# One visit per batch instead of four: grouping the value matmuls of a paged-attention loop

## The chip, the cores and the metric

The kernel runs on one core of one Trainium2 chip. Its time is the device time of one execution in microseconds (us). TensorE does the matmuls (PE in the profile, with PEld for the loads of its stationary operand), VectorE is DVE, ScalarE is ACT, GpSimd is POOL, and the queue that issues nearly all transfers is SP.

## The reference, cut to what matters

One step of a decoder layer is computed for 1024 prompt tokens and for eight samples of four new tokens each. The stage changed here is the attention of the samples over their cached past: 4096 positions in 32 pages of 128, for each of eight samples, with eight heads.

```python
def one(args):
    pages, q1, c1, pe1 = args
    c_all = jnp.concatenate([pool_ckv[pages].reshape(PAST_LEN, KV_LORA), c1.astype(pool_ckv.dtype)], axis=0)
    pe_all = jnp.concatenate([pool_kpe[pages].reshape(PAST_LEN, QK_ROPE), pe1.astype(pool_kpe.dtype)], axis=0)
    k, v = mla_keys_values(c_all, pe_all, k_pos, w_uk, w_uv, g_qk_k)
    return masked_attend(q1, k, v, q_pos, k_pos)
```

Keys are RMS-normalised per head after the projection, so each key needs the sum of squares of its 96 values. The kernel does not form the values v: it sums the cached latents with the softmax weights first and multiplies by `w_uv` once at the end.

## The kernel before

The score loop has 128 steps, 16 for each of the eight samples ("batches" 0 to 7 in the code). Four pages make a quad, so a batch has eight quads and a step handles half a quad. Everything in the loop is written out by hand in the function `steps`: for PE, ACT, DVE and POOL the order of the instructions is the order of the code, and work that belongs to a step is put there with `at(n, pos, f)`; only the order on SP is chosen by the scheduler. After step 127 a tail follows (steps 128 to 147 together with `mem_kv`, the keys and values of the prompt's memory) in which the scheduler orders every engine but SP.

In step n, `pair_score` issues 24 score matmuls into the tiles `s` and `s2` (two buffers each; both are called `s` in the profile). ACT squares both (`sq`, two buffers, lines 1452 and 1455), DVE adds the scores to `S` (line 1454) and in the next step reduces the squares to `ss` (line 1458). Every two steps ACT rounds the next quad's transposed latents to `ch` and POOL and DVE form the remainder `cl`, half each (line 1407).

The softmax of batch b runs in steps 16b+12 to 16b+21, in pieces of `batch_softmax`: sums of squares plus the rope part (line 1469) and a reciprocal root in a dozen DVE instructions on 192 columns (lines 247 to 261), the scaling of 24 pages on POOL and the peak over them on DVE, the same for the last 8 pages, then the peak over partitions: TensorE transposes `mx` (line 1508, step 16b+19), DVE reduces it and makes the diagonal `dg` (lines 1511, 1513), TensorE spreads it with `ones` (line 1516, step 16b+20), POOL subtracts, and ACT takes the exponential in step 16b+21. Batch 0 does the same while `mix_steps`, a leftover of the prompt, runs beside it.

The value matmuls come `LAG` = 4 steps after that. `quad_pv` multiplies one quad's latents `ck` by the weights in `S`. The output has 32 rows, so four pages are put into the four 32-column groups of the array; I call a run of such matmuls, between score matmuls that use the full array, a visit. An f32 matmul leaves two records in the trace, so a quad has eight records. Line 1535 adds the new tokens (`cn`) at a batch's first quad.

Before, batch b is visited in steps 16b+23, 16b+27, 16b+31 and 16b+35, with two quads each. The last of these visits stands right behind the transpose of `mx` of batch b+1. Then `batch_out` copies the sums (line 1545), divides (lines 1549 to 1555) and `batch_close` adds up the four groups (line 1561, the fold) in steps 16b+35 to 16b+39.

The latents `ck` come into a ring of 15 buffers. The same ring lends buffers to four loads of the prompt's mixer output (`mixed_load`), which ACT and DVE later scale and split into `mx0h` and `mx0l` (lines 205 and 208), one of each in two steps. POOL writes a one into each quad's column 256 (line 1284), which makes the matmul sum up the weights too.

Of the kernel before, what the change touches and what calls it, by code (L numbers as in the profile page):

```python
# [15 lines left out]
NB, ND = 8, 4  # L16
# [138 lines left out]
class Net:  # L155
# [1024 lines left out]
    def phase2b(self):  # L1180
        nc, tc, I = self.nc, self.tc, self.I
# [4 lines left out]
        ppt, pp = self.open("ps3t", space=PSUM), self.open("ps3", space=PSUM)  # L1186
# [10 lines left out]
        cosT, sinT, quads = self.cosT, self.sinT, self.quads  # L1197

        LAG, AHEAD = 4, 3
        last = NB * 16  # L1200
        st, ev, late = {}, {}, []

        def at(n, pos, f, *a):
            ev.setdefault((n, pos), []).append(lambda: f(*a))

        def run(n, pos):
            for f in ev.pop((n, pos), []):
                f()
# [13 lines left out]
        def mixed_load(k):  # L1222

            raw = place()[:, :768].rearrange("p (k n) -> p k n", k=2)
            nc.sync.dma_start(raw, self.mix_dram[:, k : k + 2, :384])
            for e in range(2):
                at(8 * k + 24 + 2 * e, 3, lambda e: self.split(*(x[:, k + e] for x in self.mx0), raw[:, e], self.col("g_ab", k + e)), e)

        for k in range(0, 8, 2):
            at(8 * k + 20, 0, mixed_load, k)  # L1230
        at(last - 4, 3, lambda: self.split(*wk0, raws[0].rearrange("p (k n) -> p k n", k=8)))
        for b in range(NB):
            n = b * 16
            at(n - 10, 0, lambda b: st.__setitem__(b, self.batch_open(p, b)), b)
            at(n - 8, 2, lambda b: self.batch_enter(st[b], b), b)
            for r, (k, pos) in enumerate(((12, 0), (13, 0), (14, 0), (14, 3) if b == NB - 1 else (15, 0), (15, 0) if b == NB - 1 else (15, 3), (16, 0), (17, 0), (17, 3), (18, 2), (19, 2), (20, 0), (20, 2), (21, 3))):
                f = lambda b=b, r=r: self.batch_softmax(p, ppt, st[b], r, b == NB - 1)
                if n + k <= last:
                    at(n + k, pos, f)
                else:  # L1240
                    late.append(f)
            if b < NB - 1:
                at(n + 21, 0, lambda b=b: self.batch_softmax(p, ppt, st[b], 13, False))
            n += 16 + LAG + 15
            tail = (
                lambda b=b: self.batch_out(pt, st[b], 0),
                lambda b=b: self.batch_out(pt, st[b], 1, ppt, b == NB - 1),
                lambda b=b: self.batch_close(pt, ppt, b, st.pop(b)),
            )
            for k, pos, f in ((0, 3, tail[0]), (2, 2, tail[1]), (3 if b == NB - 2 else 4, 3, tail[2])):  # L1250
                if b < NB - 1:
                    at(n + k, pos, f)
# [4 lines left out]
        def steps(n0, n1):  # L1257
            for n in range(n0, n1):
                Q, v = n // 2, n - 16 - LAG
                if n >= 16 and n % 2 == 0 and Q + AHEAD < NB * 8:  # L1260
                    quads[Q + AHEAD] = self.quad_load(p, Q + AHEAD)
                for k, dst, src in ((2, b4, self.b_dram), (16, self.fold4, I["c_fold4"]), (64, wuv, I["w_uv"])):
                    if n == k:
                        self.behind(nc.sync.dma_start(dst, src), self.page_dma[-1])
                if n > last - 8 and n % 2 == 0 and len(raws) < 4:
                    raw = place()[:, : 8 * P]
                    src = (I["w_mk"][0], I["memT"][:, :4], I["memT"][:, 4:], I["w_mk"][1])[len(raws)]
                    nc.sync.dma_start(raw.rearrange("p (k n) -> p k n", n=src.shape[2]), src)
                    raws.append(raw)
                for pos in (-2, -1, 0):  # L1270
                    run(n, pos)
                if n % 2 == 0 and 0 <= Q + 1 < NB * 8:
                    at(n + 1, -2, self.quad_prep(quads[Q + 1]))
                    at((6, 8, 10, 10, 11)[Q + 1] if Q < 4 else n + 3, 0, self.quad_sums, Q + 1, quads[Q + 1], st[(Q + 1) // 8])
                if n % 2 and 0 <= Q + 2 < NB * 8:
                    self.quad_rot(Q + 2, quads[Q + 2], cosT, sinT)
                if n in (-1, 1, 3, 5, 7, 9, 11, 13):
                    k = Q + 4
                    rvs[k] = rvs.get(k) or self.quad_pages(k)
                    quads[k] = self.quad_load(None, k, None, rvs[k])  # L1280
                for k in {1: (0,), 3: (1,), 4: (2,), 5: (3,), 6: (4,), 7: (5,), 9: (6,), 11: (7,), 12: (8,), 13: (9,), 14: (10,)}.get(n, ()):
                    self.quad_load(p, k, quads[k], rvs.get(k))
                if n % 2 and 0 <= v + 1 < last:
                    nc.gpsimd.memset(quads[(v + 1) // 2]["ck"][:, :, 256:257], 1.0)
                run(n, 1)
                if 0 <= n < last:
                    rope = (Q + 1, quads[Q + 1], st[(Q + 1) // 8]) if n % 2 and Q + 1 < NB * 8 else None
                    for f in self.pair_score(p, pp, n, quads[n // 2], st[n // 16], rope):
                        at(n + 1, -1, f)
                elif n == -1:  # L1290
                    self.quad_rope(self.t(pp, [P, 2, 512], F32, "s", 2)[:, 0, 320:448], 0, quads[0], st[0])()
                run(n, 2)
                if 0 <= v < last and v % 4 == 3:
                    for z in (v // 2 - 1, v // 2):
                        self.quad_pv(ppt, z, quads.pop(z), st[v // 16])
                run(n, 3)

        with tc.manual_schedule(engines={E.PE, E.Activation, E.DVE, E.Pool}):
            steps(-10, last + 1)

        with tc.manual_schedule(engines={E.SP}):
            self.close("ps3")
            for x in ("p3a", "p3c", "sq", "sm"):
                self.close(x)
            self.wr = self.open("wr", bufs=3, side="right")
            self.wp = self.open("w", bufs=3, side="right")
            mem = self.mem_kv(raws, wk0)
            for f in late[:3]:
                f()
            next(mem)  # L1310
            steps(last + 1, last + 4)
            for _ in range(5):
                next(mem)
            steps(last + 4, last + 7)
            for f in late[3:]:
                f()
            for _ in range(6):
                next(mem)
            steps(last + 7, last + 16 + LAG)
            for _ in mem:  # L1320
                pass
# [1191 lines left out]
```

## Time and profile before

| what | value |
|---|---|
| time, median of 3 runs | 1827.49 us (1826.86 to 1828.1) |
| profiled execution, from its first to its last instruction | 1823.1 us |
| TensorE busy | 1800.6 us (99%) |
| VectorE busy | 1349.6 us (74%) |
| ScalarE, GpSimd busy | 921.5 us (51%), 703.0 us (39%) |
| score loop, first score matmul to last | 400.88 to 847.28 us |

For the profiled execution the page gives the span alone; the runs' times also hold what lies around it, 4.4 us between the span and the median. Times inside the text are counted from the start of the span. A row of the timeline reads: start, duration, engine, line, operation, output<-inputs, shape, count, and in brackets the idle time of the engine before it with what ended that. A row of a table by windows reads: stretch, its length, and each engine's busy time with the number of instructions in parentheses.

### The profile page before, as it was taken

Reading aid. Unit: us, or ns where it says so; the run is one execution under the profiler, and the core shown is the slowest. Engines: PE = TensorE matmul, PEld = TensorE weight load, DVE = VectorE, ACT = ScalarE, POOL = GpSimd, SP = SyncE. Lnnn points to the kernel's source line nnn. Section 1 sums busy time; section 2 is a strip of 40 time slices with the busy share of each in tenths; the row PEclk is TensorE's granted clock in tenths of the full one; section 3 lists DMA queues with packets and bytes.
Section 4 is the critical chain, followed back from the end, with each engine's and each line's share of the span. In section 5 each row is a group of like instructions: output and inputs, shape, how many; then the busy total and the mean of one; then the engine's idle time right before and its main releaser. Section 6 shows DMA issues by size and latency. Waiting matters only on the chain.

```text
span 1823.1 us, 39307 instructions
## 1 busy us (share of the span) xinstructions
PE 1800.6 (99%) x14226; PEld 1700.3 (93%) x14226; DVE 1349.6 (74%) x2796; ACT 921.5 (51%) x1910; POOL 703.0 (39%) x861
## 2 busy tenths in 40 slices
PE   9999999999999999999999999999999999999999
PEld 8999777779999999998899979999999999999999
DVE  7864767657778776777645767998888888888664
ACT  7435676766655555556433556533333333344442
POOL 1021655534545444544023010377667776400000
PEclk9999999999999999999999999999999999999999
DMA  8102354558866766664645156222222222595242
GB/s 323 47 18 70 117 176 127 165 181 227 220 201 189 202 189 181 178 180 127 194 152 188 36 197 196 71 71 94 83 71 71 83 71 85 152 325 162 85 149 78
DMA packets 153187, 261.18 MB, mean 143 GB/s; under 512 B 20897, under 2 KB 97538, under 8 KB 152994
## 3 DMA queue, kind: packets, MB, share of 16 engines
q1 hardware_dynamic: 152130, 257.63, 45.4%
q8 instruction: 112, 1.84, 0.4%
q10 hardware_dynamic: 864, 1.05, 0.2%
q14 instruction: 81, 0.66, 0.1%
HBM read 212.79 MB, written 45.82 MB: 142 GB/s over the span
## 4 chain that ended last, share of the span: by engine, by line
PE 81%; DVE 3%; ACT 1%; issue 1%; SPq 1%; POOL 1%; DMA 0%; DVEq 0%; ACTq 0%; POOLq 0%
PE s L186 22%; PE d L186 12%; PE b L186 8%; PE F L186 7%; PE X L186 7%; PE E L186 7%; PE A L186 3%; PE y L186 3%; PE o L1047 2%; PE o L1537 2%; PE tp L1032 1%; PE tp L186 1%; PE s L1422 1%; PE tp L985 1%; PE t L186 1%
## 5 line engine op out<-in xcount | busy, mean ns | idle before, releaser
L186 PE MATMUL s<-w2h,ch 128*128 128x256 f32 x1018 | 301.9, 297 | 0.5 <-ACT S L1425 0.5
L186 PE MATMUL s<-w2h,cl 128*128 128x256 f32 x1018 | 293.2, 288 | 0.0
L186 PE MATMUL s<-w2l,ch 128*128 128x256 f32 x1018 | 292.9, 288 | 0.0
L186 PEld LDWEIGHTS s<-w2h,ch 128*128 128x128 f32 x1018 | 191.5, 188 | 8.9 <-issue 3.7
L186 PEld LDWEIGHTS s<-w2l,ch 128*128 128x128 f32 x1018 | 191.7, 188 | 0.0
L186 PEld LDWEIGHTS s<-w2h,cl 128*128 128x128 f32 x1018 | 191.3, 188 | 0.0
L1458 DVE TENSOR_REDUCE ss<-sq 128x16 f32<-128x1024 f32 x128 | 155.3, 1213 | 29.8 <-ACT sq L1455 29.4
L1407 POOL TENSOR_TENSOR cl<-cT,ch 128x512 fp32r<-128x512 f32 x64 | 83.5, 1304 | 185.6 <-ACT ch L1403 185.4
L1455 ACT ACTIVATE sq<-s 128x512 f32<-128x512 f32 x128 | 76.6, 598 | 82.7 <-PE s L186 82.7
L1452 ACT ACTIVATE sq<-s 128x512 f32<-128x512 f32 x128 | 76.9, 601 | 75.9 <-PE s L186 70.9
L201 ACT CAST a<-brb 128x528 fp32r<-128x528 f32 x77 | 48.8, 634 | 110.5 <-PE d L186 104.6
L186 PE MATMUL d<-a,w 128*128 128x264 f32 x768 | 95.2, 284 | 0.0
L202 DVE TENSOR_TENSOR a<-brb,a 128x528 fp32r<-128x528 f32 x77 | 54.1, 704 | 55.2 <-ACT a L201 55.1
L186 PEld LDWEIGHTS d<-a,w 128*128 128x128 f32 x768 | 94.3, 188 | 0.0
L2149 POOL TENSOR_TENSOR lo<-s,hi 128x1024 fp32r<-128x1024 f32 x20 | 64.0, 3200 | 45.7 <-ACT hi L2148 45.7
L186 PE MATMUL mm<-whi,xh 128*128 128x256 f32 (+3 forms) x272 | 77.1, 285 | 0.0
L2204 ACT COPY a<-A 128x264 f32<-128x264 f32 x43 | 16.1, 375 | 120.6 <-PE A L186 114.2
L186 PE MATMUL mm<-wlo,xh 128*128 128x256 f32 (+3 forms) x272 | 76.8, 285 | 0.1
L186 PE MATMUL mm<-whi,xl 128*128 128x256 f32 (+3 forms) x272 | 76.8, 286 | 0.0
L1403 ACT CAST ch<-cT 128x512 fp32r<-128x512 f32 x128 | 73.5, 629 | 0.0
L2270 POOL TENSOR_TENSOR cv<-cv,row 128x1056 f32<-128x1056 f32 x22 | 65.1, 2960 | 21.0 <-ACT cv L2269 21.0
L186 PE MATMUL d<-a,hi 128*128 128x264 f32 x552 | 72.0, 284 | 0.0
(755 smaller groups left out, 6348.1 us busy)
## 6 DMA issues: line engine op xcount, KB each, us to landing
cT<-cT SPq DMA_DIRECT2D x256, 160.0 KB, 2.8
ck<-ck SPq DMA_DIRECT2D x256, 144.0 KB, 3.4
raw<-w_up SPq DMA_DIRECT2D x44, 512.0 KB, 3.5
wsumd<-wsum SPq DMA_DIRECT2D x26, 512.0 KB, 3.9
actd<-cv SPq DMA_DIRECT2D x44, 264.0 KB, 2.4
brb<-actd SPq DMA_DIRECT2D x44, 264.0 KB, 5.7
wsum<-w_down SPq DMA_DIRECT2D x22, 512.0 KB, 3.8
raw<-wsumd SPq DMA_DIRECT2D x20, 512.0 KB, 3.7
```

The costliest lines, as they stand in the source:

```text
L186: x = self.nc.tensor.matmul(out, l, r, start=first and i == 0, stop=last and i == len(seq) - 1)
L201: first = {"act": nc.scalar.copy, "pool": nc.gpsimd.tensor_copy, "dve": nc.vector.tensor_copy}[eng](hi, src)
L202: low = lambda: nc.vector.tensor_tensor(lo, src, hi, ALU.subtract)
L1047: nc.tensor.matmul(u["o"][g : g + 64, o : o + m * P], s["v"][:, j, h % 4], th[:, z * P : (z + m) * P], start=j == 0, stop=b == len(banks) - 1,
L1403: nc.scalar.copy(d["h"][:, k], src[k])
L1407: (nc.vector if k else nc.gpsimd).tensor_tensor(d["l"][:, k], src[k], d["h"][:, k], ALU.subtract)
L1452: nc.scalar.activation(sq[:, 0], ps[:, :, n0 : n0 + 256], AF.Square)
L1455: nc.scalar.activation(sq[:, 1], pt.rearrange("p (e d) -> p e d", e=2), AF.Square)
L1458: yield lambda: nc.vector.tensor_reduce(s["ss"][:, g0 : g0 + 2].rearrange("p e (z h) -> p z e h", z=2), sq.rearrange("p z e (h d) -> p z e ...
L1537: nc.tensor.matmul(s["o"][j * 32 : j * 32 + 32], S[:, q * 4 + j], d["ck"][:, j, :257], start=q == 0 and j > 0, stop=q == 7)
L2149: eng.tensor_tensor(lo, src, hi, ALU.subtract)
L2270: nc.gpsimd.tensor_tensor(cv, cv, row, ALU.mult)
```

## The change

All eight quads of a batch are now multiplied in one visit, in step 16b+23. Batch 6 keeps two quads back: six in step 119, and two that the code places in step 131, in the tail. With the last quads done, `batch_out` and the fold follow in steps 16b+23 to 16b+27 instead of 16b+35 to 16b+39 (batch 6 keeps its place). The memset of column 256 is moved 12 steps earlier. The four mixed loads and their splits are moved four steps later: loads from steps 20, 36, 52, 68 to 24, 40, 56, 72, and splits from steps 24 and 26 (40 and 42, and so on) to 28 and 30 (44 and 46, and so on).

```diff
             for e in range(2):
-                at(8 * k + 24 + 2 * e, 3, lambda e: self.split(*(x[:, k + e] for x in self.mx0), raw[:, e], self.col("g_ab", k + e)), e)
+                at(8 * k + 28 + 2 * e, 3, lambda e: self.split(*(x[:, k + e] for x in self.mx0), raw[:, e], self.col("g_ab", k + e)), e)
 
         for k in range(0, 8, 2):
-            at(8 * k + 20, 0, mixed_load, k)
+            at(8 * k + 24, 0, mixed_load, k)
...
-            n += 16 + LAG + 15
+            n += 16 + LAG + (15 if b == NB - 2 else 3)
...
-                if n % 2 and 0 <= v + 1 < last:
-                    nc.gpsimd.memset(quads[(v + 1) // 2]["ck"][:, :, 256:257], 1.0)
+                if n % 2 and 0 <= n - 7 < last:
+                    nc.gpsimd.memset(quads[(n - 7) // 2]["ck"][:, :, 256:257], 1.0)
...
-                if 0 <= v < last and v % 4 == 3:
-                    for z in (v // 2 - 1, v // 2):
-                        self.quad_pv(ppt, z, quads.pop(z), st[v // 16])
+                if 0 <= v < last and v % 16 in (3, 15):
+                    b, held = v // 16, 2 if v // 16 == NB - 2 else 0
+                    for z in range(b * 8, b * 8 + 8 - held) if v % 16 == 3 else range(b * 8 + 8 - held, b * 8 + 8):
+                        self.quad_pv(ppt, z, quads.pop(z), st[b])
```

Here v is n - 16 - LAG. Lines behind the loop have a number one higher afterwards.

TensorE around the transpose of batch 3's peaks (step 67), before:

```order
L186 MATMUL s_1635_10295<-w2l_1706,ch_10111 128x256
L186 MATMUL s_1635_10295<-w2h_1705,cl_10112 128x256
L1508 MATMUL m_10325<-ident_60,mx_10051 32x128
L1537 MATMUL o_9494<-ck_8291,S_7186 32x257 x4
L1537 MATMUL o_9494<-ck_8434,S_7186 32x257 x4
L186 MATMUL s_10396<-w2h_1705,ch_10245 128x288
L186 MATMUL s_10396<-w2l_1706,ch_10245 128x288
```

The same place in TensorE's order afterwards:

```order
L186 MATMUL s_1638_10319<-w2l_1706,ch_10135 128x256
L186 MATMUL s_1638_10319<-w2h_1705,cl_10136 128x256
L1509 MATMUL m_10349<-ident_60,mx_10075 32x128
L186 MATMUL s_10408<-w2h_1705,ch_10269 128x288
L186 MATMUL s_10408<-w2l_1706,ch_10269 128x288
```

The eight value matmuls that stood between the transpose and the scores of step 68 are gone from there, and the transpose stands alone.

VectorE at the beginning of batch 3's softmax (steps 60 and 61), before:

```order
L1469 TENSOR_TENSOR ss_8299<-ss_8299,kss_8300 128x192
L247 TENSOR_SCALAR rqx_1578_9824<-ss_8299 128x192
L248 TENSOR_SCALAR rqy_1580_9826<-rqx_1578_9824 128x192
L249 TENSOR_SCALAR rqy_1580_9826<-rqy_1580_9826 128x192
L1454 TENSOR_TENSOR S_8298<-s_9835,S_8298 128x64
L1407 TENSOR_TENSOR cl_9832<-cT_9544,ch_9831 128x512
L1458 TENSOR_REDUCE ss_8299<-sq_9861 128x2x2x4
```

The same place in VectorE's order afterwards:

```order
L1470 TENSOR_TENSOR ss_8306<-ss_8306,kss_8307 128x192
L247 TENSOR_SCALAR rqx_1581_9852<-ss_8306 128x192
L248 TENSOR_SCALAR rqy_1583_9854<-rqx_1581_9852 128x192
L249 TENSOR_SCALAR rqy_1583_9854<-rqy_1583_9854 128x192
L1455 TENSOR_TENSOR S_8305<-s_9863,S_8305 128x64
L208 SCALAR_TENSOR_TENSOR mx0l_5691<-ck_9586,cols_58,mx0h_5690 128x384
L1408 TENSOR_TENSOR cl_9860<-cT_9574,ch_9859 128x512
L1459 TENSOR_REDUCE ss_8306<-sq_9889 128x2x2x4
```

A mixed split (line 208) now stands ahead of the remainder `cl`, and a second one does so two steps later; before, both came in the steps ahead of this stretch.

VectorE in the second half of the reciprocal root of the last batch (around step 126), before:

```order
L256 SCALAR_TENSOR_TENSOR rqa_2077_14173<-rqy_2076_14172 128x192
L259 TENSOR_TENSOR rqa_2077_14173<-rqa_2077_14173,rqx_2074_14170 128x192
L260 SCALAR_TENSOR_TENSOR rqh_2075_14171<-rqa_2077_14173 128x192
L261 SCALAR_TENSOR_TENSOR ss_12752<-rqh_2075_14171,rqy_2076_14172 128x192
L1454 TENSOR_TENSOR S_12751<-s_14263,S_12751 128x64
```

The same place in VectorE's order afterwards:

```order
L256 SCALAR_TENSOR_TENSOR rqa_2077_14187<-rqy_2076_14186 128x192
L1552 RECIPROCAL rd_14458<-m_14456 128x1
L259 TENSOR_TENSOR rqa_2077_14187<-rqa_2077_14187,rqx_2074_14184 128x192
L1556 TENSOR_SCALAR oo_14408<-oo_14408,rd_14458 128x256
L260 SCALAR_TENSOR_TENSOR rqh_2075_14185<-rqa_2077_14187 128x192
L261 SCALAR_TENSOR_TENSOR ss_12761<-rqh_2075_14185,rqy_2076_14186 128x192
L1455 TENSOR_TENSOR S_12760<-s_14277,S_12760 128x64
```

The division of batch 6's sums now stands inside the root, ahead of the last additions to `S`; before, it came after them. On TensorE the scheduler puts batch 6's two held quads not into the tail but between score matmuls of steps 122 to 126, in three pieces of 2, 2 and 4 matmuls.

## The prediction

> **What bounds the kernel now.** I read the page first, then TensorE's timeline at the visits, then VectorE's rows in the softmax steps.
>
> ```profile
> span 1823.1 us, 39307 instructions
> PE 1800.6 (99%) x14226; PEld 1700.3 (93%) x14226; DVE 1349.6 (74%) x2796; ACT 921.5 (51%) x1910; POOL 703.0 (39%) x861
> PE 81%; DVE 3%; ACT 1%; issue 1%; SPq 1%; POOL 1%; DMA 0%; DVEq 0%; ACTq 0%; POOLq 0%
> ```
>
> TensorE is busy 99% of the span and makes 81% of the chain that ended last, so an interval taken from it counts unless another engine then makes it wait. The mean hides that the engines take turns in being nearly full. A table by windows, for steps 12 to 19 of batches 0, 3 and 5, shows it:
>
> ```profile
> 439.23:466.13 26.90, 26.68 (x217) 26.47 (x215) 25.74 (x57) 15.84 (x36) 12.51 (x17) 1.00 0.86 237
> 608.26:635.77 27.51, 27.51 (x237) 25.99 (x233) 26.06 (x53) 15.12 (x32) 12.92 (x21) 1.00 0.75 218
> 721.30:748.81 27.51, 27.51 (x237) 26.00 (x234) 25.67 (x53) 14.70 (x31) 13.07 (x21) 1.00 0.60 173
> ```
>
> The fourth column is VectorE: 26.06 of 27.51 us, 95%, against 74% over the kernel. In these eight steps VectorE is almost as full as TensorE, at a granted clock of 1.00. Shorten TensorE's part here and VectorE decides.
>
> **What a visit costs.** TensorE's timeline at an ordinary visit:
>
> ```profile
> 776.58 0.28 PE L186 MATMUL s<-w2l,ch 128*128 128x256 f32 x1
> 776.70 0.28 PE L186 MATMUL s<-w2h,cl 128*128 128x256 f32 x1
> 776.91 1.07 PE L1537 MATMUL o<-ck,S 128*32 128x257 f32 x16
> 777.91 0.40 PE L186 MATMUL s<-w2h,ch 128*128 128x288 f32 x1
> 778.15 0.29 PE L186 MATMUL s<-w2l,ch 128*128 128x288 f32 x1
> 778.28 0.29 PE L186 MATMUL s<-w2h,cl 128*128 128x288 f32 x1
> ```
>
> Score matmuls start 0.12 or 0.13 apart. Across the visit it is 1.21 from 776.70 to 777.91, and the next interval is 0.24 instead of 0.13: the visit adds 1.09 + 0.11 = 1.20 us. The one visit with four quads tells how much of that is work:
>
> ```profile
> 847.28 0.28 PE L186 MATMUL s<-w2h,cl 128*128 128x256 f32 x1
> 847.49 1.94 PE L1537 MATMUL o<-ck,S 128*32 128x257 f32 x32
> 850.23 0.36 PE L1605 MATMUL b<-mh,wk0h 128*128 128x256 f32 x1 [0.80 <-DVE S L1454]
> ```
>
> Thirty-two records take 1.94 where sixteen take 1.07, so two more quads inside a visit cost 0.87, or 0.054 per record. Entering and leaving costs 1.20 - 0.87 = 0.33. Batches 0 to 5 lose three visits each: 18 x 0.33 = 5.9 us saved. The adding of the new tokens stays once per batch, and the fold moves with unchanged count, both at nothing. ACT's copy of the sums (line 1545) now waits for the end of the long visit, and behind it on ACT stand the rope copy and the rounding of a quad that TensorE wants only two steps later; TensorE makes no scores meanwhile, so this is covered, and were it not, step 26 of the cycle would begin late by the excess.
>
> One of three visits stood behind the transpose of the peaks, which itself has 32 output columns and now stands alone. Batch 0 has that already, with no visit before it in its whole softmax; TensorE, VectorE and POOL there:
>
> ```profile
> 465.98 0.28 PE L186 MATMUL s<-w2h,cl 128*128 128x256 f32 x1
> 466.10 0.27 PE L1508 MATMUL m<-ident,mx 128*32 128x128 f32 x1
> 466.13 0.38 PE L186 MATMUL s<-w2h,ch 128*128 128x288 f32 x1
> 470.19 0.40 PE L1516 MATMUL m<-dg,ones 32*128 32x32 f32 x2 [0.81 <-DVE dg L1513]
> 467.84 1.21 DVE L1458 TENSOR_REDUCE ss<-sq 128x16 f32<-128x1024 f32 x1
> 468.97 0.27 DVE L1511 TENSOR_REDUCE mm<-m 32x1 f32<-32x128 f32 x1
> 469.27 0.86 DVE L1513 TENSOR_SCALAR dg<-ident,mm 32x32 f32<-32x32 f32 x1
> 468.83 1.27 POOL L1407 TENSOR_TENSOR cl<-cT,ch 128x512 fp32r<-128x512 f32 x1 [1.01 <-ACT ch L1403]
> ```
>
> The lone transpose begins 0.12 after a score matmul and the next begins 0.03 after it: no overhead of 0.33. I charge nothing. [...]
>
> **The wait that comes instead.** The same rows show what the visits hid. Without one, TensorE waited 0.81 for `dg`. Batch 3, with visits:
>
> ```profile
> 632.19 0.19 DVE L1505 TENSOR_TENSOR mx<-mx 128x32 f32<-128x32 f32 x1
> 635.40 1.22 DVE L1458 TENSOR_REDUCE ss<-sq 128x16 f32<-128x1024 f32 x1 [0.69 <-ACT sq L1455]
> 636.84 0.23 DVE L1513 TENSOR_SCALAR dg<-ident,mm 32x32 f32<-32x32 f32 x1
> 634.57 0.27 PE L1508 MATMUL m<-ident,mx 128*32 128x128 f32 x1
> 634.77 1.07 PE L1537 MATMUL o<-ck,S 128*32 128x257 f32 x16
> 638.99 0.40 PE L1516 MATMUL m<-dg,ones 32*128 32x32 f32 x2
> ```
>
> `dg` is done at 637.07 and used at 638.99: 1.92 us to spare. Three visits leave ahead of that point (steps 59, 63, 67), so TensorE comes 3.6 us sooner. VectorE can follow only where it idles: 0.69 before its row at 635.40, and about 0.2 at the start of the stretch, where it waits for squares. So 3.6 - 0.2 - 1.92 - 0.69 = 0.8 us of new wait per batch. Behind `m<-dg` the scores of the next step are queued on TensorE, and behind those everything.
>
> Onto the same eight steps of batches 1 to 4 the change moves two mixed splits each:
>
> ```profile
> L208 DVE SCALAR_TENSOR_TENSOR mx0l<-ck,cols,mx0h x8: 618/620/839, 486.4 to 661.9; 128x384 fp32r<-128x384 f32 x8
> ```
>
> Two at 0.62 to 0.84, some 1.3 together, with VectorE full from there to the peak: 0.8 + 1.3 = 2.1 us for each of four batches, 8.4. Where the wait shows (scores waiting for `cl` or for the addition to `S`, the transpose for `mx`, or `m<-dg`) is open; the slip is one. Batches 5 and 6 have no split, and VectorE does 26.06 - 25.67 = 0.4 less there: 0.4 each, 0.8. Together 9.2 us. From below, a mixed batch waits as batch 0 does, 0.81, and the other two not at all: 3.2 us; a gain is excluded, since VectorE's work grows and its time shrinks. From above stand these rows of VectorE and POOL:
>
> ```profile
> 609.33 1.25 DVE L1469 TENSOR_TENSOR ss<-ss,kss 128x192 f32<-128x192 f32 x1
> 616.57 1.29 POOL L1407 TENSOR_TENSOR cl<-cT,ch 128x512 fp32r<-128x512 f32 x1 [4.64 <-ACT ch L1403]
> 616.71 1.36 DVE L256 SCALAR_TENSOR_TENSOR rqa<-rqy 128x192 f32<-128x192 f32 x1
> 619.33 2.08 POOL L1476 TENSOR_TENSOR S<-S,ss 128x768 f32<-128x768 f32 x1 [1.47 <-DVE ss L261]
> ```
>
> A VectorE instruction begun 0.14 after POOL's ran until 0.21 after POOL's end. The second split comes just when POOL begins its 2.08 us scaling. If that gets in between split and `cl`, `cl` loses up to 1.6: 3.7 for a mixed batch; and `dg` may take 0.86 as in batch 0 rather than 0.23, 1.0 for the others. That end is 4 x 3.7 + 2 x 1.0 = 16.8. I take 9.2, since batch 3's rows are nearest to the batches changed.
>
> **Batch 6 and the tail.** By the end of step 123 TensorE has done 54 records of batch 6 instead of 34; 20 x 0.054 = 1.1 us more. It gets nothing back: these records filled TensorE until VectorE's addition at 849.87, and it waited 0.80 even so.
>
> ```profile
> 849.87 0.21 DVE L1454 TENSOR_TENSOR S<-s,S 128x64 f32<-128x64 f32 x1
> 851.52 0.16 DVE L1551 RECIPROCAL rd<-m 128x1 f32<-128x1 f32 x1
> 852.48 0.35 DVE L1555 TENSOR_SCALAR oo<-oo,rd 128x256 f32<-128x256 f32 x1
> 854.70 3.87 POOL L263 TENSOR_TENSOR rqa<-rqy 128x64 f32<-128x64 f32 x1 [2.94 <-DVE rqy L249]
> 867.06 0.27 PE L1508 MATMUL m<-ident,mx 128*32 128x128 f32 x1 [0.22 <-DVE mx L1505]
> ```
>
> The last softmax is a chain over VectorE and POOL to 867.06, where TensorE already waits. The division (0.16 + 0.35) now stands ahead of that addition: 0.5 us later. Freed fold work only lengthens TensorE's waits. Between 0 and 1.5 for this term; I take 0.5.
>
> The earlier memsets are covered by POOL's 39%. SP's wait for buffers is this:
>
> ```profile
> SPq L1379 <- PE o L1537: 21.4, 11, 7.0
> ```
>
> Up to 7.0 us, with loads issued seven steps ahead of the first reader. Quads now leave no later than before, so SP waits no longer and the mixed loads, four steps later but with four steps kept to their splits, cost nothing; were that cover gone, a late transposed tile would show as ACT waiting.
>
> **Sum**: -5.9 + 9.2 + 1.1 + 0.5 = +4.9 us on 1823.1, so 1828.0 for the span; the median lies 4.4 above the span, giving 1832.4 for the runs.
>
> **Rivals.**
> - VectorE slips no further than in batch 0: 3.2 us of waits, -5.9 + 3.2 + 1.6 = -1.1, 1826.4. For it: batch 0's measured 0.81, with extra work of its own. Against it: batch 0 has no splits here.
> - Faster: VectorE keeps up everywhere. Place: `dg` of batches 1 to 6; price: all 9.2 us; it decides if the slip of 3.4 to 4.7 us falls under 1.92 + 0.69 = 2.6. That needs VectorE's stretched rows, such as 1.25 at 609.33, to shrink because they meet POOL elsewhere. Then -5.9 + 1.6 = -4.3, 1823.2. Against it: VectorE's 95%.
> - POOL's scaling gets ahead of `cl`: 16.8 us of waits, +12.5, 1839.9. [...]
>
> **How the numbers follow.** About 0.2%, 3.65 us, can be told from no change. Forecast 0.43, slip as in batch 0 0.34 (counted as the same), faster 0.12, POOL first 0.11. Slower is 0.43 + 0.11 = 0.54. The range 1824.5 to 1838.5 leaves out the ends of the second and third rivals, some 0.1 on either side; the forecast's own is 1831.2 to 1837.
>
> **What would show it.** One visit of 66 records per batch of about 4 us (66 x 0.054 + 0.33 = 3.9), score matmuls 0.12 apart where visits were, and idle before TensorE's scores, transpose or `m<-dg` in steps 28 to 36 of each cycle, released by VectorE, larger in batches 1 to 4 than in 5 and 6. I am wrong if VectorE's rows shrink, if TensorE's idle there stays under 3 us in sum, or if a lone transpose pays 0.33.

## The result, and the profile after

The changed kernel takes 1838.38 us (median of 5 runs, 1835.61 to 1840.22) where the kernel before takes 1826.95 (5 runs, 1825.14 to 1828.1): a ratio of 1.0058, 95% interval 1.0046 to 1.0069. The forecast was 1832.4; the third rival, POOL's scaling in the way of `cl`, stood at 1839.9. In the changed kernel the lines behind 1295 are one higher: `cl` is line 1408, the addition to `S` 1455, the reduction of squares 1459, POOL's scaling 1477, the transpose 1509, `dg` 1514 and 1517, the value matmuls 1538.

The page first: its span, its busy times, the chain that ended last, and the one group of score matmuls that waits.

```profile
span 1836.2 us, 39334 instructions
PE 1800.3 (98%) x14226; PEld 1703.4 (93%) x14226; DVE 1359.8 (74%) x2796; ACT 918.8 (50%) x1910; POOL 703.8 (38%) x861
PE 71%; DVE 10%; ACT 2%; issue 2%; SPq 2%; DMA 1%; POOL 1%; DVEq 0%; ACTq 0%; POOLq 0%
L186 PE MATMUL s<-w2h,cl 128*128 128x256 f32 x1018 | 294.5, 289 | 6.8 <-DVE cl L1408 6.8
```

TensorE's busy time is that of before (1800.6), and 13.1 us of span were added. The busy time did not fall with the visits: a matmul's record lasts some 0.28 us where the next one normally starts 0.12 after it, so short waits count as busy, and so does slower work (in two rows of the last section, 20 records fill 4.00 us at a granted clock of 0.57 where 31 fill 3.88 at 1.00). VectorE's share of the chain goes from 3% to 10%. The last number of the group names a place: 6.8 us of waits for `cl`, of which the page of before had none.

The table by windows for steps 12 to 19 of batches 1, 3 and 5 of the changed kernel, columns as before:

```profile
497.87:526.49 28.62, 26.89 (x204) 26.65 (x203) 27.37 (x52) 15.92 (x35) 13.18 (x21) 0.94 0.64 180
615.94:643.46 27.52, 25.72 (x203) 25.25 (x203) 26.28 (x51) 15.71 (x35) 13.20 (x21) 1.00 0.62 179
733.83:758.93 25.10, 25.10 (x203) 25.09 (x203) 23.86 (x49) 14.92 (x33) 13.06 (x21) 1.00 0.66 181
```

In batch 3 the stretch is as long as it was with visits in it (27.51), although TensorE is busy 1.8 us less (25.72): the time of the visits has turned into idle time. In batch 5, which has no splits, it is 25.10.

Where TensorE idles, in batch 3. VectorE, POOL and TensorE at the end of step 63 and the start of step 64:

```profile
627.71 0.36 DVE L261 SCALAR_TENSOR_TENSOR ss<-rqh,rqy 128x192 f32<-128x192 f32 x1
627.98 0.21 DVE L1455 TENSOR_TENSOR S<-s,S 128x64 f32<-128x64 f32 x1
628.12 2.00 DVE L208 SCALAR_TENSOR_TENSOR mx0l<-ck,cols,mx0h 128x384 fp32r<-128x384 f32 x1
630.04 0.94 DVE L1408 TENSOR_TENSOR cl<-cT,ch 128x512 fp32r<-128x512 f32 x1
628.14 1.56 POOL L1477 TENSOR_TENSOR S<-S,ss 128x768 f32<-128x768 f32 x1 [1.47 <-DVE ss L261]
629.01 0.29 PE L186 MATMUL s<-w2l,ch 128*128 128x288 f32 x1
631.03 0.40 PE L186 MATMUL s<-w2h,cl 128*128 128x288 f32 x1 [1.74 <-DVE cl L1408]
```

The second split takes 2.00 us, where the splits of before took 0.62 to 0.84. It began 0.02 before POOL's scaling and ended 0.42 after it; `cl` stands behind it on VectorE, and TensorE waits 1.74 for `cl`. I call an instruction held when its row is stretched past the end of the other engine's. The four second splits all read 2.00, each 0.02 to 0.03 ahead of the scaling, since both follow the last instruction of the reciprocal root (line 261): POOL waits for its result, and on VectorE only the short addition to `S` stands between it and the split.

And the transpose and `dg` of the same batch, TensorE, VectorE, POOL:

```profile
643.32 0.28 PE L186 MATMUL s<-w2h,cl 128*128 128x256 f32 x1
643.43 0.27 PE L1509 MATMUL m<-ident,mx 128*32 128x128 f32 x1
643.46 0.38 PE L186 MATMUL s<-w2h,ch 128*128 128x288 f32 x1
643.68 0.30 PE L186 MATMUL s<-w2l,ch 128*128 128x288 f32 x1
645.39 1.20 DVE L1459 TENSOR_REDUCE ss<-sq 128x16 f32<-128x1024 f32 x1
646.51 0.27 DVE L1512 TENSOR_REDUCE mm<-m 32x1 f32<-32x128 f32 x1
646.82 0.85 DVE L1514 TENSOR_SCALAR dg<-ident,mm 32x32 f32<-32x32 f32 x1
646.36 1.28 POOL L1408 TENSOR_TENSOR cl<-cT,ch 128x512 fp32r<-128x512 f32 x1 [2.86 <-ACT ch L1404]
647.73 0.40 PE L1517 MATMUL m<-dg,ones 32*128 32x32 f32 x2 [0.99 <-DVE dg L1514]
```

TensorE waits 0.99 for `dg`. Two things stand in its way: it comes behind the reduction of squares of the step before (1.20), and it takes 0.85 instead of 0.23, ending 0.03 after POOL's `cl`, inside which it began. In the batches 0 to 6 `dg` takes 0.85 to 0.86 throughout.

From here on I compare kernels by one stretch, from the first score matmul of step 32 to that of step 96: four cycles, three visits fewer per cycle. Three of the four pairs of splits lie in it; the first pair begins ahead of it, but the wait that follows that pair in the changed kernel (step 32) lies inside. Before and after, the rows of a table by windows (the third column is TensorE's busy time):

```profile
508.88:734.95 226.07, 226.07 (x1904) 212.72 (x1901) 169.26 (x327) 131.85 (x291) 107.63 (x173) 1.00 0.67 190
```

```profile
510.40:746.36 235.96, 225.88 (x1902) 215.48 (x1901) 178.11 (x329) 130.25 (x290) 111.54 (x173) 0.99 0.64 178
```

226.07 became 235.96: 9.9 of the 13.1 us lie here, with 10.1 us of idle TensorE.

### The profile page after: what moved, and what is told of

Same layout as the page of the kernel before. It is cut to its first block, busy times and chain, and to the rows that moved or that the text cites. A ratio compares the mean times of both kernels' runs of the same rounds, so it can differ in the third digit from the quotient of the medians.

```text
span 1836.2 us, 39334 instructions
## 1 busy us (share of the span) xinstructions
PE 1800.3 (98%) x14226; PEld 1703.4 (93%) x14226; DVE 1359.8 (74%) x2796; ACT 918.8 (50%) x1910; POOL 703.8 (38%) x861
## 4 chain that ended last, share of the span: by engine, by line
PE 71%; DVE 10%; ACT 2%; issue 2%; SPq 2%; DMA 1%; POOL 1%; DVEq 0%; ACTq 0%; POOLq 0%
PE s L186 13%; PE d L186 12%; PE b L186 8%; PE F L186 7%; PE X L186 7%; PE E L186 7%; PE A L186 3%; PE y L186 3%; DVE ss L1459 3%; PE o L1047 2%; PE o L1538 1%; PE tp L1032 1%; PE tp L186 1%; DVE cl L1408 1%; SPq L1380 1%
## 5 line engine op out<-in xcount | busy, mean ns | idle before, releaser
L1455 DVE TENSOR_TENSOR S<-s,S 128x64 f32<-128x64 f32 x128 | 27.9, 218 | 68.7 <-ACT sq L1453 68.7
```

The costliest lines, as they stand in the source:

```text
L1455: nc.vector.tensor_tensor(S, ps[:, :, sc : sc + 32], S, ALU.add)
```

## Experiments

**Splits put back.** The changed kernel, with

```diff
-                at(8 * k + 28 + 2 * e, 3, lambda e: self.split(...), e)
+                at(8 * k + 24 + 2 * e, 3, lambda e: self.split(...), e)
-            at(8 * k + 24, 0, mixed_load, k)
+            at(8 * k + 20, 0, mixed_load, k)
```

> The changed kernel with the mixed loads and splits in their old steps (loads at 8k+20, splits at 8k+24 and 8k+26); the grouped visits and earlier folds stay. In the changed kernel TensorE waits 1.7 us for cl in step 32 of the cycle of batches 1 to 4, some 0.4 at the score addition and 1.0 for dg, 3.3 us per batch; batches 5 and 6, without splits, wait 0.65 and 0.85. Theory 1 (the second split, begun 0.02 us before POOL's scaling, is held for 2.00 us and makes cl late): the wait for cl goes, batches 1 to 4 wait 0.6 to 0.9 for dg alone, 4 x 2.5 = 10 us less: 1828 (1826 to 1830). Theory 2 (VectorE is late because the visits are gone, and the split only marks where it shows): a wait of 1 us or more stays at cl or at the score addition in batches 1 to 4: 1833 or more.

1827.8 us against 1825.9 of the kernel before, run beside it; ratio 1.0008 (95% interval 0.9999 to 1.0017). The stretch:

```profile
512.16:737.61 225.45, 222.40 (x1902) 213.54 (x1901) 168.71 (x327) 130.91 (x290) 107.03 (x173) 1.00 0.66 186
```

and from its table of groups, in the score loop, `m<-dg` with its idle time last:

```profile
L1517 PE MATMUL m<-dg,ones 32*128 32x32 f32 x14 | 2.8, 282 | 5.8 <-DVE dg L1514 5.8
```

The stretch is 10.5 us shorter than with the splits moved, no wait for `cl` is left, and 5.8 us of waits for `dg` are (0.58 to 1.00 in each of batches 0 to 6). That is theory 1: the moving of the splits is what made the change slower; without it, the saved visits and the waits for `dg` come out even.

**Splits alone moved**, in the kernel before (the same two lines of the diff, nothing else).

> The kernel before with the mixed loads and splits alone moved four steps later; visits and folds as before. Theory 1 (the held split costs only because no visit gives VectorE time): the second split takes 2.0 us here too, but TensorE reaches the step 2.3 us later, so cl has 2.4 us to spare and dg 1.9: waits of 0 to 0.4 per batch, 1827 to 1829. Theory 2 (the held split costs its time wherever it stands): 1.4 to 2.0 for each of four batches, 1832.5 to 1835.

1830.67 us, ratio 1.0027 (1.0018 to 1.0036). The stretch:

```profile
510.20:741.36 231.16, 228.57 (x1904) 213.42 (x1900) 179.80 (x332) 130.35 (x292) 113.23 (x175) 1.00 0.66 185
```

and the group of scores that waits:

```profile
L186 PE MATMUL s<-w2h,cl 128*128 128x256 f32 x1018 | 293.8, 289 | 2.3 <-DVE cl L1407 2.3
```

Between the theories: 5.1 us on the stretch, 1.3 per batch, where I expected 0 to 0.4 and the rival 1.4 to 2.0. The split is held for 2.00 here too, and the visits cover part of it: the waits for `cl` are 0.8 and 0.5 instead of 1.7. Only 2.6 of the 5.1 show as idle time (231.16 - 228.57); the rest is waits that count as busy. At the end of step 34, for one, the matmul `s<-bd,krq` starts 0.34 after the score ahead of it (520.65, 520.99), where it is 0.12 in the version with both mends further down. My estimate of 2.4 us to spare was too large.

**Splits kept apart**, in the changed kernel:

```diff
-                at(8 * k + 28 + 2 * e, 3, lambda e: self.split(...), e)
+                at(8 * k + 28 + e, 3, lambda e: self.split(...), e)
```

> The changed kernel with the second split of a pair one step after the first (8k+28 and 8k+29 instead of 8k+28 and 8k+30), so that cl and not a split stands on VectorE when POOL's scaling begins. The amount of VectorE's work is the same. [...] Theory 2 (VectorE is simply full): the lost time stays 3.3 per batch, shown at the addition or at dg: 1837 or more.

1828.82 us, ratio 1.0015 (1.0005 to 1.0024), where I had expected 1831 to 1835 if neither split is held. The stretch:

```profile
510.94:739.15 228.21, 224.18 (x1902) 214.05 (x1901) 170.24 (x328) 130.29 (x290) 110.33 (x173) 1.00 0.66 184
```

and VectorE and POOL in batch 3, with the second split one step earlier:

```profile
620.97 0.61 DVE L208 SCALAR_TENSOR_TENSOR mx0l<-ck,cols,mx0h 128x384 fp32r<-128x384 f32 x1
622.63 0.83 DVE L256 SCALAR_TENSOR_TENSOR rqa<-rqy 128x192 f32<-128x192 f32 x1
624.70 0.68 DVE L1408 TENSOR_TENSOR cl<-cT,ch 128x512 fp32r<-128x512 f32 x1
624.72 2.08 POOL L1477 TENSOR_TENSOR S<-S,ss 128x768 f32<-128x768 f32 x1 [1.47 <-DVE ss L261]
```

The same two splits, 7.8 us less on the stretch. The split takes 0.61; `cl` now meets the scaling, and here POOL is the one stretched (2.08 for 1.56). Two splits in these steps cost 228.21 - 225.45 = 2.8 us against the splits put back, 0.7 per batch, where the forecast had 1.3; the whole slip, against the version with both mends (222.09), is 1.5 per batch and not the 2 us I still expected. Part of the difference can be seen: begun later, an instruction of the root (line 256) meets less of POOL's `cl` (0.62 us of it instead of 1.15) and takes 0.83 (1.37 in the changed kernel), half a microsecond less.

**Split behind `cl`**, in the changed kernel:

```diff
-                at(8 * k + 28 + 2 * e, 3, lambda e: self.split(...), e)
+                at(8 * k + 28 + 3 * e, -1 if e else 3, lambda e: self.split(...), e)
```

> The changed kernel with the second split of each pair placed behind VectorE's cl of step 31 of the cycle instead of in front of it. cl is then the instruction that begins with POOL's scaling, and the split begins some 0.7 us into the scaling. [...] Theory 2 (the split was slow only by starting together with the scaling): 0.6 to 0.8 us, and 1828 to 1830.

1835.87 us, ratio 1.0051 (1.0035 to 1.0066), a little above the 1831 to 1835 that I had expected if the split is held again. The stretch:

```profile
510.08:744.52 234.44, 225.31 (x1903) 214.26 (x1902) 176.52 (x329) 129.82 (x290) 111.79 (x173) 1.00 0.64 182
```

VectorE and POOL in batch 2:

```profile
568.47 0.68 DVE L1408 TENSOR_TENSOR cl<-cT,ch 128x512 fp32r<-128x512 f32 x1
569.07 1.93 DVE L208 SCALAR_TENSOR_TENSOR mx0l<-ck,cols,mx0h 128x384 fp32r<-128x384 f32 x1
568.50 2.09 POOL L1477 TENSOR_TENSOR S<-S,ss 128x768 f32<-128x768 f32 x1 [1.47 <-DVE ss L261]
```

and a group of TensorE that waits now, 4.3 us where it was 0.5 in the changed kernel:

```profile
L1423 PE MATMUL s<-bd,krq 128*128 128x128 f32 x128 | 26.2, 286 | 4.3 <-ACT S L1426 4.0
```

`cl` is on time and no score waits for it. The split is held again, to 0.41 after POOL's end, so the wait moves to the next thing that needs VectorE: ACT's copy of the rope part, which stands behind the addition to `S`, and the matmul that needs its buffer. Only 1.5 of 10.5 us come back. So the holding costs here too, at another place in VectorE's order.

**`dg` early**, in the changed kernel: the pieces `mm` and `dg` of `batch_softmax` ahead of the reduction of squares. Of the one long line that changes, the part in question:

```diff
-(18, 2), (19, 2), (20, 0), (20, 2), (21, 3)
+(18, 2), (19, 2), (20, -2), (20, 2), (21, 3)
```

> The changed kernel with the reduction to mm and the making of dg moved ahead of the reduction of squares of the step before (1.21 us), in every batch. In the changed kernel dg begins 0.45 us after POOL's cl and lasts 0.85 us, and TensorE waits 0.6 to 1.0 for it in batches 0 and 2 to 6, 5.3 in sum. Theory 1 (dg is late by its place on VectorE and by POOL's cl, not by VectorE's fullness): dg takes 0.23, ends 1.7 us sooner, the wait for dg is under 0.1 everywhere, and at most 0.3 per batch comes back at the next cl: 1834 (1833 to 1836). Theory 2 (VectorE bounds the whole stretch): the wait turns up at the next cl or addition: 1837 to 1839. The waits for cl in step 32 stay 1.7 under both.

1831.58 us, ratio 1.0033 (1.0022 to 1.0043). The stretch:

```profile
509.68:741.38 231.70, 224.63 (x1902) 214.12 (x1901) 176.25 (x329) 129.27 (x290) 112.14 (x173) 1.00 0.65 185
```

`dg` from 400 to 850 us (least, median and largest duration in ns):

```profile
L1514 DVE TENSOR_SCALAR dg<-ident,mm x7: 228/228/229, 469.1 to 811.6; 32x32 f32<-32x32 f32 x7
```

and the group of `m<-dg` in the score loop:

```profile
L1517 PE MATMUL m<-dg,ones 32*128 32x32 f32 x14 | 2.8, 282 | 0.0
```

No wait for `dg` is left and nothing comes back at the next `cl`; the time is even below theory 1's range. The two possible causes of the late `dg`, its place and POOL's `cl`, went together in this run, and I did not part them.

**Both mends**, splits back and `dg` early, on the changed kernel.

> Both mends together on the changed kernel: splits in their old steps, and mm and dg ahead of the reduction of squares of the step before. With the splits back, TensorE waited for dg alone, 5.8 us in sum over batches 0 to 6 (0.6 to 1.0 each), at 1827.8. Theory 1 (all that is left of the loss is dg's place): these waits go and nothing takes their place: 1822 (1820.5 to 1823.5), 0.2% under the kernel before at 1825.9, which is the saving of the grouped visits laid bare (18 visits fewer). Theory 2 (VectorE is full in these steps, so another wait comes): waits of 0.5 or more at cl or at the score addition in most batches: 1825 to 1828.

1821.3 us (1819.02 to 1822.96) against 1826.74, ratio 0.9962 (0.9949 to 0.9976): faster than both kernels.

```profile
510.81:732.90 222.09, 222.09 (x1902) 213.55 (x1901) 167.11 (x327) 130.10 (x290) 107.59 (x173) 1.00 0.68 193
```

TensorE is busy for the whole stretch, as before the change: VectorE now keeps up without the visits. The stretch is 226.07 - 222.09 = 3.98 us shorter: twelve visits fewer, 0.33 each.

**The same with four quads of batch 6 held.**

> The same with four quads of batch 6 held instead of two. In the changed kernel TensorE waits 1.5 us before the first b<-mh for VectorE's last score addition, 0.8 in the kernel before, which had four quads left there. Theory 1 (records kept back fill that wait): 0.7 us less than with two held, about 1821.3. Theory 2 (the held records go out in small pieces between the last score steps, each of which pays its entry, and none lands in the wait): 0.5 to 1.5 us more, 1822.5 to 1823.5.

1820.58 us, ratio 0.9966 (0.9954 to 0.9978): not to be told from the run above, so neither theory's difference shows. The wait of 1.5 us ahead of the first `b<-mh` stays; the held records went out ahead of it.

**`dg` early in the kernel before.**

> The kernel before with mm and dg ahead of the reduction of squares, nothing else. Theory 1 (dg's place costs only where no visit covers it): batch 0's wait of 0.8 us goes and the other batches, with 1.9 us to spare, stay as they are: 1825.1 against 1825.9, not to be told from no change. Theory 2 (dg early is a gain of its own in every batch): 3 us or more, under 1823.

1825.44 us against 1826.74, ratio 0.9989 (0.9980 to 0.9999).

```profile
505.96:732.04 226.08, 226.08 (x1905) 212.75 (x1901) 170.14 (x327) 131.96 (x291) 107.70 (x174) 1.00 0.66 188
```

The stretch is unchanged (226.07), so an early `dg` is worth nothing there while visits cover it; only batch 0's wait is gone. The gain of the mended version is the grouping's.

**Scaling later on POOL**, in the changed kernel, alone and with `dg` early (again a part of the one long line):

```diff
-(14, 3) if b == NB - 1 else (15, 0), (15, 0) if b == NB - 1 else (15, 3)
+(14, 3) if b == NB - 1 else (15, 1), (15, 0) if b == NB - 1 else (15, 3)
```

> The changed kernel with POOL's scaling of step 31 of the cycle put behind the rope products and the memset of the same step (1.4 us of POOL's work that was idle-free to start earlier); VectorE's and TensorE's orders are unchanged, and the split still stands in front of cl. [...] Theory 2 (the split's place in front of cl is enough to make cl late): a split of 0.6 still leaves 0.5 us or more of wait at cl: 1833 or more.

> The whole change kept, with two mends in the order alone: POOL's scaling as in the run above, and mm and dg ahead of the reduction of squares. Theory 1: no wait is left in the score loop and the time is that of the version with the splits moved back, 1821.3 (1820 to 1823.5). Theory 2 (two splits more in the softmax steps cost VectorE's time whatever holds them): 0.6 us for each of four batches more than that, 1823.7, or more.

1842.03 us, ratio 1.0081 (1.0059 to 1.0104), above the 1838 that I expected if the split stays held, and 1832.01, ratio 1.0028 (1.0016 to 1.0041), the latter no better than `dg` early alone. VectorE and POOL of the first:

```profile
628.35 0.50 DVE L259 TENSOR_TENSOR rqa<-rqa,rqx 128x192 f32<-128x192 f32 x1
629.42 0.50 DVE L261 SCALAR_TENSOR_TENSOR ss<-rqh,rqy 128x192 f32<-128x192 f32 x1
629.98 1.99 DVE L208 SCALAR_TENSOR_TENSOR mx0l<-ck,cols,mx0h 128x384 fp32r<-128x384 f32 x1
630.00 1.55 POOL L1477 TENSOR_TENSOR S<-S,ss 128x768 f32<-128x768 f32 x1 [0.25 <-DVE ss L261]
```

The edit missed its aim. The rope products now ran beside the root on VectorE and stretched it (0.50 for 0.36), so POOL was done with them before `ss` was ready, and the scaling again began 0.02 after the split. The run does not tell how much head start a split needs. A row of the kernel before tells something, with another POOL instruction: there a split began at 486.42, 0.12 ahead of POOL's `krq` (line 1392), and ran its 0.62, while POOL took 0.83 (median 0.47).

## Why the prediction was right and wrong

- **Direction**: slower, as forecast: visits go, VectorE is late in the softmax steps, TensorE waits. But VectorE was late mainly through its order and through POOL: with both mends, which also take two splits out of these steps, it keeps up, as the second rival had it, and TensorE never idles in the stretch. No run has the splits in these steps, none of them held, together with an early `dg`. 1838.38 lies above the forecast's own 1831.2 to 1837 and 0.12 under the upper end of the range, with two of the five runs above that end (1838.92, 1840.22). That it came out inside is luck.
- **Visits**, -5.9 at 0.33 each: right. With the waits mended, twelve visits are worth 3.98 us. The visit itself took 4.2 us rather than the forecast 3.9: 4.11 from the score at 598.57 to the next at 602.80, less one interval of 0.12, and 0.11 because the interval behind it is longer. If entering and leaving cost 0.33 and the 64 records of the quads 0.054 each, 0.4 is left for the two of the new tokens, which come once per batch in both kernels.

```profile
598.57 0.28 PE L186 MATMUL s<-w2h,cl 128*128 128x256 f32 x1
598.78 0.40 PE L1536 MATMUL o<-cn,S 128*32 128x257 f32 x1
599.03 3.84 PE L1538 MATMUL o<-ck,S 128*32 128x257 f32 x61
602.80 0.40 PE L186 MATMUL s<-w2h,ch 128*128 128x288 f32 x1
603.03 0.29 PE L186 MATMUL s<-w2l,ch 128*128 128x288 f32 x1
```

- **Lone transpose**, 0: nearly right. It starts 0.11 behind a score and 0.03 ahead of the next (643.43, 643.46), and the interval behind that is 0.22 instead of 0.13: some 0.1 in all, and not 0.33.
- **Waits**, 9.2: this is the term that was mis-sized; with the 0.7 and 0.8 of batches 5 and 6 below, they come to 15.4, near the upper end of 16.8. On the stretch of four mixed batches the changed kernel loses 235.96 - 222.09 = 13.9 us against the version with both mends, 3.5 per batch, where I had 2.1 and an upper end of 3.7; 10.1 of it show as idle time (235.96 - 225.88). The step that failed is "two at 0.62 to 0.84": I priced the splits by rows in which POOL hardly met them, though I had written that the second comes just when POOL begins its scaling. Held, it takes 2.00. The third rival had the meeting, the place (`cl`) and nearly the price (1.6; the split lost 1.4), but the wrong victim: not `cl` behind the scaling, but the split behind it and `cl` behind the split. I gave it 0.11. Begun 0.02 ahead of the scaling, `cl` runs its 0.68 (splits kept apart), and a split takes 2.00. The 1.3 that I did charge for two splits is 0.7 when nothing holds them (splits kept apart).
- **`dg`**: I took 0.8 of slip and left `dg` at its 0.23, with 0.86 in the upper end. All of batches 1 to 6 got 0.85. With the splits put back, the waits for `dg` in batches 1 to 6 are 0.58 to 0.92, near the 0.8 that I had for the slip alone; but `dg` lasts 0.62 longer there than I reckoned, so that figure came near by luck. In batches 5 and 6, forecast 0.4 each, TensorE waited 0.6 and 0.8. By windows:

```profile
746.36:802.76 56.40, 55.81 (x478) 53.59 (x476) 41.85 (x81) 31.94 (x71) 27.65 (x44) 1.00 0.64 178
```

```profile
732.90:788.61 55.71, 55.71 (x477) 53.58 (x476) 41.60 (x81) 31.72 (x71) 27.70 (x44) 1.00 0.63 181
```

Above are steps 96 to 111, first of the changed kernel, then of the version with both mends: 0.69 us is what late `dg` costs a batch that has no splits.
- **Batch 6 and tail**, 1.1 + 0.5: about right. The last transpose comes at 878.27 against 867.06, 11.2 us later, and -5.9 + 15.4 + 1.6 is 11.1. The score loop's last step had come 12.35 later (856.64 against 844.29): the tail, with fewer records left in it, gave 1.1 back, and TensorE's wait for the last addition grew from 0.80 to 1.52, as the prediction said it would.

```profile
861.78 0.35 PE L1606 MATMUL b<-mh,wk0h 128*128 128x256 f32 x1 [1.52 <-DVE S L1455]
878.27 0.27 PE L1509 MATMUL m<-ident,mx 128*32 128x128 f32 x1 [0.43 <-DVE mx L1506]
```

- **Behind the last transpose**, at nothing: 958.0 us follow it in the changed kernel (878.27 to 1836.2) and 956.0 in the kernel before (867.06 to 1823.1). The difference, 1.9 of the 13.1 us of span, goes with a dip of the clock in the tail, of which more below.
- **Outside the span**, 4.4: a step that mixed two executions. In the changed kernel the execution of span 1836.2 took 1838.38, so 2.2 lie outside. In the later runs of the kernel before, 1.7 do (1824.83 for a span of 1823.1), so its profiled execution took some 1824.8, an estimate, 2.7 under the median that the forecast started from; that part of the 4.4 was the difference between executions. The errors add up: 1832.4 + 6.2 for the waits + 1.9 for the dip + 0.1 for the rest - 2.2 outside the span is 1838.4.

## What to carry to other kernels

A VectorE instruction had no price of its own here (a split took 0.61 to 2.00 us): ask what POOL does in the same microsecond, above all where both follow the same instruction, since then they meet in every repetition. Work that is grouped to save switching can also take away the pauses in which another engine caught up; find what stood behind each pause, and move that first (here one piece of the softmax ahead of one reduction, and two splits left where they were, turned +0.6% into -0.4%).

## What the runs showed of the hardware

Who is held when VectorE and POOL meet was not decided here by the first start alone. `cl` (TENSOR_TENSOR) and the split (SCALAR_TENSOR_TENSOR) both began 0.02 us ahead of the same scaling: `cl` ran its 0.68 and POOL took 2.08, while the split took 2.00 and POOL 1.56. The splits were held, ending 0.42 after POOL there and 0.41 after it with the split behind `cl`, where it began 0.57 into the scaling. What decides who is held, and why one of the two is held at all, the runs do not show.

TensorE's granted clock falls to half for some 3.4 us at a time, or twice as long (6.9 us in the kernel before: 0.60 from 215 to 219 and 0.54 from 219 to 223), up to three times in one of these profiles (its last 3 us left aside), at places that differ between them. Three stretches of the changed kernel, with the clock as the third number from the right:

```profile
513.00:517.00 4.00, 4.00 (x20) 4.00 (x21) 3.97 (x6) 1.80 (x4) 2.47 (x6) 0.57 0.73 186
572.00:576.00 4.00, 3.88 (x31) 3.88 (x32) 4.00 (x6) 2.45 (x6) 2.46 (x5) 1.00 0.67 178
885.00:889.00 4.00, 4.00 (x12) 3.12 (x11) 2.18 (x13) 1.40 (x2) 0.00 (x0) 0.57 0.35 99
```

A mean of 0.57 over 4.00 us is 3.4 us at half clock (0.43 x 4.00 / 0.5); a stretch that lies wholly in such a dip, 215 to 219 of the run with the splits put back, reads 0.50. The first dip above follows the 1.73 us wait for `cl` of batch 1; the second stretch follows the 1.67 us wait of batch 2 and is at full clock; the third lies in the tail. Half of 3.4 is 1.7 us of TensorE's work, an estimate. The profiles have 1.5 to 2.1: the time from the last transpose to the end of the span is 956.0 to 956.1 in the six without a dip there, and 957.6 to 958.1 in the six with one, the changed kernel among them. The dip in batch 1 hardly cost anything in the end, since VectorE caught up and that batch then did not wait for `dg`.

Whether a wait sets off a dip stays open: three waits like that of batch 1 (1.67, 1.74 and 1.68 us in batches 2 to 4) have none behind them, and in the version with both mends, whose stretch has neither a wait nor a dip, dips come elsewhere (0.50 from 215 to 219, 0.62 from 235 to 239, 0.69 from 868 to 872).
